# One-bank PSUM tiles instead of two-bank tiles for the accumulators of a gated MLP

## The chip, the cores and the metric

The kernel runs on one core of one Trainium2 chip. The core has five engines that run side by side and meet through semaphores: TensorE (matrix multiplication, "PE" in the profile), VectorE ("DVE"), ScalarE ("ACT"), GpSimd ("POOL") and SyncE ("SP", which issues transfers). TensorE writes its sums to PSUM, a memory of 8 banks; in this kernel a bank holds 512 fp32 values in each of 128 partitions. The metric is the device time of one execution in microseconds, as the median of several runs. Before the change it is 2559.89 us (three runs, 2557.91 to 2560.74).

## What is computed

One layer of a diffusion transformer over 512 latent tokens with 256 context tokens, in fp32: a modulated RMS norm, two attention mixers, an output projection, and a gated MLP, then a final norm. The change lies in the MLP, whose gate passes a convolution of width 3 over the tokens:

```python
g, u = jnp.split(h @ w_up, 2, axis=-1)            # h: 512 x 2048, w_up: 2048 x 11264
gp = jnp.pad(g, ((0, 0), (pad, pad), (0, 0)))
g = sum(gp[:, j:j + T] * conv_w[j] for j in range(CONV_W)) + conv_b
return (jax.nn.silu(g) * u) @ w_down              # w_down: 5632 x 2048
```

## The kernel before, in words

Tokens lie along the free dimension (T = 512 columns, halves h0 and h1 of HT = 256), features along the 128 partitions. Every fp32 product is made of three matmuls (`mm3`, L99 to L104): operands are split into a high part ("wh", cast on ScalarE) and the remainder ("wl", subtracted on VectorE), and high times high, high times low and low times high are added up in PSUM.

The 5632 features of the MLP are 44 tiles of 128. A tile needs two blocks of results, its gate g and its linear part u. Tiles 0 and 1 are made in `first_pair`, tile 2 by four plain jobs "u", the tiles 3 to 43 (`PAIRS`) by seven jobs each, ("p", ft, 0) to ("p", ft, 6), in a scheme of the Strassen kind: seven products of half size (8 weight blocks of 128 x 128 by 256 columns, 3 matmuls each, so 24 matmuls a job) take the place of eight. "A pair" in what follows is such a pair of g and u, one ft. Its seven products go to three accumulators: k = 0 to y, 1 to x, 2 to y, 3 to z, 4 to y, 5 to z, 6 to y. Readers take intermediate sums from them between the jobs:

- L999, ScalarE, after k = 0: copies y to m1
- L1002, ScalarE, after k = 2: copies y to u2
- L1005, ScalarE, and L1028, VectorE, after k = 3: copy z to m5, and g[h0] = x + m1
- L1033, VectorE, after k = 4: u[h1] = y + m5
- L1035, VectorE, after k = 5: u[h0] = z + u2
- L1007, ScalarE, after k = 6: copies y to g[h1]; then the convolution, SiLU and product with u (L806 to L828) follow, spread over the next pair's jobs

The down projection is spread among these jobs: after every fourth pair its 16 output blocks come in eight jobs "d", each of 24 matmuls with 512 columns into two PSUM tiles "b", at the places `DOWN_AFTER` (7, 8, 10, 11, 13, 14, 16, 17), counted as (ft % 4) * 7 + k. Their results go through ScalarE (L992, tile xs) and are added to the stream in DRAM by GpSimd's queue (L993).

The order is written out by hand (`manual_schedule`, L900) for TensorE, ScalarE, VectorE and SyncE, each a strict queue in this order (L1041 to L1055): for step i, the matmuls of job i are issued (`run`), then a sum of weight blocks where one is due (`weight_sum`, VectorE), the cast of the weights of job i + 2 (L945, ScalarE), the readers of job i - 1 (`act_after` on ScalarE, `vec_after` on VectorE), and the low part of the weights of job i + 2 (L951, VectorE). Weights come in by SyncE's queue in two rings of three buffers (L869).

The semaphores are not written by hand: the framework derives the waits from what each instruction reads and writes. A pool hands out tiles; tiles of one tag rotate through `bufs` buffers. Before the change PSUM is shared by two pools: `ps_s` (L60) with two tiles "s" of two banks, which has served since the kernel's start, and `ps_c` (L650) with four tiles "b" of one bank. A pair takes one tile s (L969): y is the first half of its first bank, z and x are the two halves of its second. Tile 2's jobs "u" use one tile s, g in its first bank and u in its second (L961).

Of the kernel before, what the change touches and what calls it, by code (L numbers as in the profile page):

```python
# [15 lines left out]
PSUM = bass.MemoryType.PSUM  # L16
# [36 lines left out]
def layer_kernel(ctx: ExitStack, tc: tile.TileContext, small, rope, c_row, cc_row, x_t, ctx_t, ada, ada_k,  # L53
# [3 lines left out]

    cst = ctx.enter_context(tc.tile_pool(name="cst", bufs=1))
    dram = ctx.enter_context(tc.tile_pool(name="dram", bufs=1, space=bass.MemoryType.DRAM))
    ps_s = ctx.enter_context(tc.tile_pool(name="ps_s", bufs=2, space=PSUM))  # L60
    ps_b = tc.alloc_tile_pool(name="ps_b", bufs=4, space=PSUM)

    n = [0]
# [5 lines left out]
    def s_tile():  # L69
        return ps_s.tile([P, 1024], F32, tag="s", name=nm("s"))  # L70
# [576 lines left out]
    mc.release()  # L647
    rp.release()
    ps_b.release()
    ps_b = ctx.enter_context(tc.tile_pool(name="ps_c", bufs=4, space=PSUM, reuse_waits="tile"))  # L650


    HT = T // 2
# [64 lines left out]
    db = sm.tile([P, 8], F32, name="db")  # L718
    ve.tensor_tensor(db, modx[:, 56:64], modx[:, 48:56], op=ALU.add)
    wo.release()  # L720

# [176 lines left out]
    with tc.manual_schedule(engines={mybir.EngineType.PE, mybir.EngineType.Activation, mybir.EngineType.DVE,  # L900
                                     mybir.EngineType.SP}):
        ra, rb = Ring(wp, "wr", 3, items_a), Ring(mm, "rb", 3, items_b)
        sums_, ready, live = {}, {}, {}

        def small(tag):
            return mm.tile([P, HT], F32, tag=tag, name=nm(tag), bufs=1)

        def weight_sum(ft, i):

            if ft >= NFT:  # L910
                return
            w12, w21, w22 = (rb.tiles.get((k, ft)) for k in ("w12", "w21", "w22"))
            if i in (1, 2):
                sums_[ft, i] = mm.tile([P, 1024], F32, tag="ws", name=nm("ws"), bufs=2)
            if i == 1:
                ve.tensor_tensor(sums_[ft, 1], w12, ra.tiles["w11", ft], op=ALU.subtract)
                ra.used(("w11", ft))
            elif i == 2:
                ve.tensor_tensor(sums_[ft, 2], w22, sums_[ft, 1], op=ALU.subtract)
                rb.used(("w22", ft))  # L920
            elif i == 3:
                ve.tensor_tensor(w12, w22, w12, op=ALU.subtract)
                rb.used(("w12", ft))
                rb.used(("w22", ft))
            else:
                ve.tensor_tensor(sums_[ft, 2], w21, sums_[ft, 2], op=ALU.subtract)
                rb.used(("w21", ft))

        def operand(job):

            if job[0] != "p":
                return ra.tiles[job], lambda: ra.used(job)
            ft, k = job[1:]
            if k == 0:
                return ra.tiles["w11", ft], lambda: ra.used(("w11", ft))
            if k in (2, 3, 6):
                return sums_[ft, 1 if k == 3 else 2], None
            key = ({1: "w21", 4: "w12", 5: "w22"}[k], ft)
            return rb.tiles[key], lambda: rb.used(key)

        def cast(i):
            if i < last:
                raw, done = operand(jobs[i])
                hi, lo = (wp.tile([P, 1024], F32R, tag=g, name=nm(g), bufs=3) for g in ("wh", "wl"))
                sc.copy(hi, raw)  # L945
                ready[i] = hi, lo, raw, done

        def low(i):
            if i < last:
                hi, lo, raw, done = ready[i]  # L950
                ve.tensor_tensor(lo, raw, hi.bitcast(F32), op=ALU.subtract)  # L951
                if done:
                    done()

        def run(i):
            job = jobs[i]
            wh, wl = ready.pop(i)[:2]
            w = [(wh[:, j * P:(j + 1) * P], wl[:, j * P:(j + 1) * P]) for j in range(8)]
            if job[0] == "u":
                if job[1] == 0:  # L960
                    live["s"] = s_tile()  # L961
                o = live["s"][:, (job[1] // 2) * 512:(job[1] // 2) * 512 + 512]
                for j in range(8):
                    kt = (job[1] % 2) * 8 + j
                    classical(o, kt, w[j], kt == 0, kt == KT - 1)
            elif job[0] == "p":
                ft, k = job[1:]
                if k == 0:
                    s = s_tile()  # L969
                    live[ft] = {"y": s[:, :HT], "z": s[:, 512:512 + HT], "x": s[:, 512 + HT:]}  # L970
                hs, out, start = ((h11, "y", True), (h21, "x", True), (t2, "y", False), (t1, "z", False),
                                  (t3, "y", False), (t4, "z", False), (h22, "y", False))[k]
                for j in range(8):
                    mm3(live[ft][out], w[j], hs[j], start and j == 0, j == 7, True)
            else:
                live["po"] = []
                for d in range(2):
                    po = b_tile()
                    for f in range(FC):
                        mm3(po, w[f * 2 + d], acts[job[1] * FC + f], f == 0, f == FC - 1)  # L980
                    live["po"].append(po)

        def act_after(i):

            job = jobs[i]
            if job[0] == "u" and job[1] == 3:
                live["t"] = gate_in(2, live["s"][:, :512])
            elif job[0] == "d":
                for d, po in enumerate(live["po"]):
                    dt = job[2] * 2 + d  # L990
                    x = mm.tile([P, T], F32, tag="xs", name=nm("xs"), bufs=XS)
                    sc.mul(x, po, modx[:, 80 + dt:81 + dt])  # L992
                    gp.dma_start(x1_d[dt], x, accum_op=ALU.add)  # L993
            elif job[0] == "p":
                ft, k = job[1:]
                v = live[ft]
                if k == 0:
                    v["m1"] = small("m1")
                    sc.copy(v["m1"], v["y"])  # L999
                elif k == 2:  # L1000
                    v["u2"] = small("u2")
                    sc.copy(v["u2"], v["y"])  # L1002
                elif k == 3:
                    v["m5"] = small("m5")
                    sc.copy(v["m5"], v["z"])  # L1005
                elif k == 6:
                    sc.copy(v["g"][:, h1], v["y"])  # L1007
                    v["t"] = gate_in(ft, v["g"])

        def vec_after(i):  # L1010
            job = jobs[i]
            if job[0] == "u" and job[1] == 3:
                silu(convolve(2, live["s"][:, :512], live["t"]))
            elif job == ("p", 3, 0):
                acts[2] = multiply(live["t"], live["s"][:, 512:])
            elif job == ("p", 3, 1):
                finish(live["t"], acts[2])
            if job[0] != "p":
                return
            ft, k = job[1:]  # L1020
            v, f = live[ft], live.get(ft - 1)
            if k == 2 and f:
                silu(convolve(ft - 1, f["g"], f["t"]))
            elif k == 3:
                if f:
                    acts[ft - 1] = multiply(f["t"], f["u"])
                v["g"] = mm.tile([P, T], F32, tag="g", name=nm("g"), bufs=1)
                ve.tensor_tensor(v["g"][:, h0], v["x"], v["m1"], op=ALU.add)  # L1028
            elif k == 4:
                if f:  # L1030
                    finish(f["t"], acts[ft - 1])
                v["u"] = mm.tile([P, T], F32, tag="u", name=nm("u"), bufs=1)
                ve.tensor_tensor(v["u"][:, h1], v["y"], v["m5"], op=ALU.add)  # L1033
            elif k == 5:
                ve.tensor_tensor(v["u"][:, h0], v["z"], v["u2"], op=ALU.add)  # L1035

        cast(0)
        low(0)
        cast(1)
        low(1)  # L1040
        for i, job in enumerate(jobs):  # L1041
            run(i)
            if job[0] == "p":
                ft, k = job[1:]
                if k in (0, 1, 2):
                    weight_sum(ft, k + 2)
                elif k == 6:
                    weight_sum(ft + 1, 1)
            elif job == ("u", 3):
                weight_sum(3, 1)  # L1050
            cast(i + 2)
            if i:
                act_after(i - 1)
                vec_after(i - 1)
            low(i + 2)  # L1055
        act_after(last - 1)
        f = live[NFT - 1]
        silu(convolve(NFT - 1, f["g"], f["t"]))
        acts[NFT - 1] = finish(f["t"], multiply(f["t"], f["u"]))
# [104 lines left out]
```

## Time and profile before

| | us |
|---|---|
| median of three runs | 2559.89 |
| lowest, highest | 2557.91, 2560.74 |
| the profiled execution | 2557.82 |
| its span (first to last instruction) | 2556.0 |
| TensorE matmul busy | 2420.2 |
| VectorE, ScalarE, GpSimd busy | 1643.2, 1087.3, 245.3 |

The profile is one execution. A line of its timeline reads: start and duration in us, engine, line of the kernel, operation, result <- operands (names of tiles without their numbers), shape, and in brackets how long the engine had been idle and whose end let it go on. A table of stretches gives, for each stretch of time, its length and the busy time of every engine with the number of instructions, then the granted clock of TensorE (1.00 is full), the share of the transfer engines and GB/s. Matmuls are pipelined: one is drawn longer than the distance to the next.

### The profile page before, as it was taken

What the parts mean: (1) busy time and instruction counts of PE and PEld (TensorE: products, weight loads), DVE (VectorE), ACT (ScalarE), POOL (GpSimd) and SP (SyncE); (2) the same over time, 40 slices, a digit from 0 to 9 for tenths busy, and PEclk for the clock granted to TensorE, in tenths of its full rate; (3) what the DMA queues carried; (4) which work ended last, traced back from release to release, by engine and by line L of the source; (5) the groups of instructions that cost most, each with busy time, mean ns of one, the idle gap of its engine ahead of it and who ended that gap; (6) DMA issues with size and microseconds to landing.
All of it is one profiled execution on the core that took longest, in us unless ns stands there. A gap on an engine that the chain in (4) does not pass through costs nothing.

```text
span 2556.0 us, 37051 instructions
## 1 busy us (share of the span) xinstructions
PE 2420.2 (95%) x14948; PEld 2104.7 (82%) x14948; DVE 1643.2 (64%) x2102; ACT 1087.3 (43%) x1660; POOL 245.3 (10%) x266
## 2 busy tenths in 40 slices
PE   7999999999899999999999999999999999999996
PEld 3778887777677788788989888988898889888886
DVE  4778876498787874675564646464646465656556
ACT  4342221365555622344444444444444444444443
POOL 0000000211100012000101010101010101010103
PEclk8999999999999999999999999999999999999998
DMA  7868888544311196224546363636363636454554
GB/s 276 289 211 321 328 331 303 174 130 135 111 41 46 66 335 220 96 97 118 133 114 151 93 163 100 161 97 161 102 146 108 150 100 147 118 134 127 136 165 149
DMA packets 131874, 407.78 MB, mean 160 GB/s; under 512 B 14451, under 2 KB 25203, under 8 KB 123251
## 3 DMA queue, kind: packets, MB, share of 16 engines
q1 hardware_dynamic: 106422, 356.11, 41.5%
q0 software_dynamic: 25280, 49.30, 11.0%
q8 instruction: 117, 1.92, 0.3%
q14 instruction: 55, 0.45, 0.1%
HBM read 335.88 MB, written 69.48 MB: 159 GB/s over the span
## 4 chain that ended last, share of the span: by engine, by line
PE 82%; DVE 8%; ACT 5%; issue 1%; DMA 1%; POOL 1%; SPq 0%; ACTq 0%; DVEq 0%; POOLq 0%
PE s L102 14%; PE s L103 13%; PE s L104 13%; PE b L103 10%; PE b L102 10%; PE b L104 10%; PE s L480 2%; ACT wh L945 2%; PE f L102 1%; PE pt L492 1%; DVE m L482 1%; PE f L103 1%; PE f L104 1%; DVE p L538 1%; PE b L217 1%
## 5 line engine op out<-in xcount | busy, mean ns | idle before, releaser
L102 PE MATMUL s<-a2k,wh 128*128 128x256 f32 (+1 forms) x1536 | 461.3, 301 | 24.9 <-DVE u L1033 16.4
L103 PE MATMUL s<-a2k,wh 128*128 128x256 f32 (+1 forms) x1536 | 458.9, 299 | 0.0
L104 PE MATMUL s<-a2k,wl 128*128 128x256 f32 (+1 forms) x1536 | 458.9, 299 | 0.0
L102 PEld LDWEIGHTS s<-a2k,wh 128*128 128x128 f32 x1536 | 293.9, 192 | 40.8 <-DVE u L1033 14.4
L103 PEld LDWEIGHTS s<-a2k,wh 128*128 128x128 f32 x1536 | 294.2, 192 | 9.0 <-issue 1.4
L104 PEld LDWEIGHTS s<-a2k,wl 128*128 128x128 f32 x1536 | 294.0, 191 | 8.5 <-DVE wl L951 0.8
L102 PE MATMUL b<-ah,wh 128*128 128x512 f32 (+1 forms) x768 | 286.3, 374 | 3.7 <-ACT ah L824 2.6
L103 PE MATMUL b<-al,wh 128*128 128x512 f32 (+1 forms) x768 | 287.0, 374 | 0.0
L104 PE MATMUL b<-ah,wl 128*128 128x512 f32 (+1 forms) x768 | 285.7, 372 | 0.0
L993 POOL DMA_DIRECT2D x_d<-xs x160 | 139.7, 1001 | 1258.9 <-ACT xs L992 1256.9
L78 ACT CAST wh<-wr 128x1024 fp32r<-128x1024 f32 (+2 forms) x134 | 132.7, 991 | 268.6 <-PE b L104 84.4
L951 DVE TENSOR_TENSOR wl<-ws,wh 128x1024 fp32r<-128x1024 f32 x123 | 150.4, 1223 | 136.6 <-ACT wh L945 136.6
L79 DVE TENSOR_TENSOR wl<-wr,wh 128x1024 fp32r<-128x1024 f32 (+2 forms) x134 | 156.6, 1169 | 104.3 <-ACT wh L78 100.7
L951 DVE TENSOR_TENSOR wl<-wr,wh 128x1024 fp32r<-128x1024 f32 x125 | 151.7, 1220 | 110.7 <-ACT wh L945 110.5
L945 ACT CAST wh<-rb 128x1024 fp32r<-128x1024 f32 x123 | 129.4, 1052 | 218.4 <-PE s L103 95.7
L945 ACT CAST wh<-wr 128x1024 fp32r<-128x1024 f32 x125 | 131.4, 1051 | 212.5 <-PE b L103 127.5
L945 ACT CAST wh<-ws 128x1024 fp32r<-128x1024 f32 x123 | 128.9, 1048 | 198.7 <-PE s L103 145.9
L951 DVE TENSOR_TENSOR wl<-rb,wh 128x1024 fp32r<-128x1024 f32 x123 | 150.1, 1221 | 96.8 <-ACT wh L945 96.8
L169 DVE CUSTOM_DVE_ANT_0 ada<-ada,cb,smt 128x2048 f32<-128x2048 f32 x64 | 151.2, 2365 | 58.7 <-DMA ada<-in_ada 58.4
L103 PE MATMUL s<-b2k,wh 128*128 128x256 f32 x656 | 185.6, 283 | 0.0
L102 PE MATMUL s<-b2k,wh 128*128 128x256 f32 x656 | 185.6, 283 | 0.0
L104 PE MATMUL s<-b2k,wl 128*128 128x256 f32 x656 | 185.4, 283 | 0.0
(317 smaller groups left out, 5450.7 us busy)
## 6 DMA issues: line engine op xcount, KB each, us to landing
ada<-in_ada SPq DMA_DIRECT2D x64, 1024.0 KB, 6.6
rb<-in_w_up SPq DMA_DIRECT2D x123, 512.0 KB, 4.3
wr<-in_w_dn SPq DMA_DIRECT2D x96, 512.0 KB, 3.2
x_d<-xs POOLq DMA_DIRECT2D x160, 256.0 KB, 5.9
wr<-in_w_up SPq DMA_DIRECT2D x53, 512.0 KB, 3.7
wr<-in_w_f SPq DMA_DIRECT2D x34, 512.0 KB, 6.2
adak<-in_ada_k SPq DMA_DIRECT2D x32, 512.0 KB, 6.2
ada<-in_ada SPq DMA_DIRECT2D x32, 512.0 KB, 6.5
```

The costliest lines, as they stand in the source:

```text
L78: sc.copy(dst_h, src)
L79: ve.tensor_tensor(dst_l, src, dst_h.bitcast(F32), op=ALU.subtract)
L102: pe.matmul(out, st[0], mv[0], start=start, stop=False, **kw)
L103: pe.matmul(out, st[0], mv[1], start=False, stop=False, **kw)
L104: pe.matmul(out, st[1], mv[0], start=False, stop=stop, **kw)
L169: ve.tensor_tensor_reduce(out=junk, in0=w, in1=vec, op0=ALU.mult, op1=ALU.add, scale=1.0, scalar=col("b_ada", j), accum_out=dst[:, j:j + 1])
L217: pe.matmul(acc[32 * c:32 * c + 32, :n], cpad[:, kt], src(kt), start=j == 0, stop=j == 3)
L480: pe.matmul(s[:, c0:c1], a, b[:, c0:c1], start=i == 0, stop=i == len(mms) - 1)
L482: ve.tensor_reduce(out=m, in_=s[:, :TT], axis=AX.X, op=ALU.max, negate=True)
L945: sc.copy(hi, raw)
L951: ve.tensor_tensor(lo, raw, hi.bitcast(F32), op=ALU.subtract)
L993: gp.dma_start(x1_d[dt], x, accum_op=ALU.add)
```

## The change

The MLP's accumulators become tiles of one bank each, from tags "y" and "z" with two buffers; x stays in z's bank. To make room the two PSUM pools are released after the output projection, and one new pool, `ps_m`, holds all eight banks: four tiles b, two y, two z. Jobs, matmuls, readers and their order stay as they are.

```diff
-    ps_s = ctx.enter_context(tc.tile_pool(name="ps_s", bufs=2, space=PSUM))
+    ps_s = tc.alloc_tile_pool(name="ps_s", bufs=2, space=PSUM)
...
-    ps_b = ctx.enter_context(tc.tile_pool(name="ps_c", bufs=4, space=PSUM, reuse_waits="tile"))
+    ps_b = tc.alloc_tile_pool(name="ps_c", bufs=4, space=PSUM, reuse_waits="tile")
...
     wo.release()
+    ps_b.release()
+    ps_s.release()
+    ps_b = ctx.enter_context(tc.tile_pool(name="ps_m", bufs=4, space=PSUM, reuse_waits="tile"))
...
                 if job[1] == 0:
-                    live["s"] = s_tile()
-                o = live["s"][:, (job[1] // 2) * 512:(job[1] // 2) * 512 + 512]
+                    live["s"] = [b_tile(g_, 2) for g_ in "yz"]
+                o = live["s"][job[1] // 2]
...
                 if k == 0:
-                    s = s_tile()
-                    live[ft] = {"y": s[:, :HT], "z": s[:, 512:512 + HT], "x": s[:, 512 + HT:]}
+                    y, z = (b_tile(g_, 2) for g_ in "yz")
+                    live[ft] = {"y": y[:, :HT], "z": z[:, :HT], "x": z[:, HT:]}
...
-                live["t"] = gate_in(2, live["s"][:, :512])
+                live["t"] = gate_in(2, live["s"][0])
...
-                silu(convolve(2, live["s"][:, :512], live["t"]))
+                silu(convolve(2, live["s"][0], live["t"]))
...
-                acts[2] = multiply(live["t"], live["s"][:, 512:])
+                acts[2] = multiply(live["t"], live["s"][1])
```

## The prediction

> **What bounds the kernel now.** I read the page first (busy shares, clock), then the waits of TensorE, then the timeline around one of those waits, then a table of stretches.
>
> ```profile
> span 2556.0 us, 37051 instructions
> PE 2420.2 (95%) x14948; PEld 2104.7 (82%) x14948; DVE 1643.2 (64%) x2102; ACT 1087.3 (43%) x1660; POOL 245.3 (10%) x266
> ```
>
> TensorE sets the time: 95% busy, VectorE next with 64%. So only what stands between matmuls can be won. The waits of TensorE, longest first (in total us, times, longest), begin with four rows, all ahead of a matmul into tile s, the MLP's accumulator:
>
> ```profile
> PE s L102 <- DVE g L1028: 18.4, 20, 0.9
> PE s L102 <- DVE u L1033: 16.4, 30, 0.6
> PE s L102 <- ACT m L999: 10.8, 21, 0.5
> PE s L102 <- ACT u L1002: 9.7, 21, 0.5
> ```
>
> Together 55.3 us in 92 waits. What they wait for are readers of the accumulator. A pair of tiles runs seven jobs of 24 matmuls, k = 0 to 6, into y, x, y, z, y, z, y (L971); y fills the first bank of s, z and x the halves of the second. After job i+1 is issued, the readers of job i's sum are (L1052 to L1054). The timeline at the end of job 1 of pair 3 (start, duration, engine, line, idle before and what ended it):
>
> ```profile
> 1143.12 0.28 PE L103 MATMUL s<-a2k,wh 128*128 128x256 f32 x1
> 1143.24 0.28 PE L104 MATMUL s<-a2k,wl 128*128 128x256 f32 x1
> 1143.55 0.37 ACT L999 COPY m<-s 128x256 f32<-128x256 f32 x1 [0.97 <-PE s L104]
> 1143.98 0.39 PE L102 MATMUL s<-tp,wh 128*128 128x256 f32 x1 [0.46 <-ACT m L999]
> 1144.20 0.28 PE L103 MATMUL s<-tp,wh 128*128 128x256 f32 x1
> 1144.32 0.29 PE L104 MATMUL s<-tp,wl 128*128 128x256 f32 x1
> ```
>
> L999 copies y, which job 0 had finished 24 matmuls (2.9 us) earlier. ScalarE stood idle for 0.97 us and began 0.03 us after the last matmul of job 1, which writes x, in the other bank. Then job 2, which writes y, waited for the copy. So a reader waits for everything already issued into its two-bank tile, not only for its own bank. Where a job of the down projection (tile b) comes between, it doesn't wait:
>
> ```profile
> 1715.63 0.28 PE L104 MATMUL s<-a2k,wl 128*128 128x256 f32 x1
> 1715.75 0.40 PE L102 MATMUL b<-ah,wh 128*128 128x512 f32 x1
> ...
> 1716.45 0.40 PE L102 MATMUL b<-ah,wh 128*128 128x512 f32 x1
> 1716.68 0.39 PE L103 MATMUL b<-al,wh 128*128 128x512 f32 x1
> 1716.91 0.39 PE L104 MATMUL b<-ah,wl 128*128 128x512 f32 x1
> 1717.14 0.39 PE L102 MATMUL b<-ah,wh 128*128 128x512 f32 x1
> ```
>
> ```profile
> 1715.83 1.05 ACT L945 CAST wh<-wr 128x1024 fp32r<-128x1024 f32 x1 [0.66 <-PE s L103]
> 1716.79 0.36 ACT L999 COPY m<-s 128x256 f32<-128x256 f32 x1
> ```
>
> Here the same copy follows its predecessor on ScalarE at once, at 1716.79, while matmuls into b run. They keep their 0.23 us from start to start through the copy, so such a read costs TensorE nothing visible.
>
> **The change part by part.** With y and z as tiles of their own, a reader of y waits for the last job into y alone. Five reads change (the job they wait for now, in brackets): L999 (1), L1002 (3), L1005 and L1028 (4), L1033 (5), L1035 (6). Nobody waits for L1035. The other four hold up the next job; which pairs have them follows from DOWN_AFTER. Down jobs follow k = 0, 1, 3, 4, 6 in pairs with ft % 4 = 1 and k = 0, 2, 3 in those with ft % 4 = 2. That leaves all four stalls in the 21 pairs with remainder 0 or 3 (3, 4, 7, 8, ... 43), and L1033's alone in 10 pairs with remainder 2: 31. The counts of the waits (20, 30, 21, 21) are these, short by one record in two rows.
>
> What a stall costs is more than its row. Unstalled matmuls of 256 columns start every 0.12 us, though each is drawn 0.28 long, so idle counted from the drawn end leaves out 0.16; and the second matmul after a stall starts 0.22 after the first, 0.10 more. In the rows above: 1143.24 to 1144.20 is 0.96, unstalled 0.24, so 0.72 against a wait of 0.46. First sum: 55.3 + 92 x 0.26 = 79.2 us. Second sum, from one pair without down jobs, cut from one L1002 to the next:
>
> ```profile
> core 0: us, PE busy (x) PEld busy (x) DVE busy (x) ACT busy (x) POOL busy (x), PEclk, DMA share, GB/s
> 1678.04:1701.64 23.60, 21.18 (x169) 20.37 (x168) 16.56 (x19) 10.18 (x14) 0.00 (x0) 1.00 0.28 91
> ```
>
> Its 168 matmuls take 168 x 0.12 = 20.16 us; 23.60 - 20.16 = 3.44 is lost. 21 x 3.44 = 72.2, plus 10 x (0.6 + 0.26) = 8.6 for the pairs with L1033 alone (0.6 is that row's longest): 80.8. I take **80 us**.
>
> Does something else come next? Three reads need to be done by the time the next job into their bank begins, one whole job (24 x 0.12 = 2.88 us) later: L999 and L1002 stand on ScalarE behind one cast of 1.05 us, L1033 on VectorE. The narrowest is L1028, which reads x behind L1005's read of z, and job 5 then writes z:
>
> ```profile
> 1678.16 0.37 ACT L1002 COPY u<-s 128x256 f32<-128x256 f32 x1 [1.95 <-PE s L104]
> 1678.43 0.64 ACT L818 ACTIVATE t<-t 128x512 f32<-128x512 f32 x1
> 1678.96 1.04 ACT L945 CAST wh<-ws 128x1024 fp32r<-128x1024 f32 x1
> 1681.76 0.37 ACT L1005 COPY m<-s 128x256 f32<-128x256 f32 x1 [1.75 <-PE s L104]
> ```
>
> ```profile
> 1679.10 0.69 DVE L822 TENSOR_TENSOR t<-t,u 128x512 f32<-128x512 f32 x1 [0.98 <-ACT t L818]
> 1682.16 0.42 DVE L1028 TENSOR_TENSOR g<-s,m 128x256 f32<-128x256 f32 x1 [2.38 <-ACT m L1005]
> ```
>
> After the change L1002 and L818 move into job 3, so the cast can start with job 4, when its buffer comes free (the cast at 1715.83 above began 0.08 us after the matmuls of the next job): 1.05 + 0.37 + 0.42 and three hand-overs of about 0.05 (1681.76 + 0.37 to 1682.16 is 0.03) give L1028's end 2.0 us into job 4, 0.9 before job 5. L822, ahead of it on VectorE, comes earlier as L818 does. If that cover is gone, this stall stays:
>
> ```profile
> 1681.44 0.28 PE L104 MATMUL s<-b2k,wl 128*128 128x256 f32 x1
> 1682.64 0.39 PE L102 MATMUL s<-tp,wh 128*128 128x256 f32 x1 [0.92 <-DVE g L1028]
> ```
>
> 1.20 from start to start, 1.08 more than unstalled, and 0.10 for the second matmul: 21 x 1.18 = 25 us. As a whole VectorE has 16.6 us of work in a pair of 20.2, ScalarE 10.2. The transfers of such a pair, 91 GB/s now, become 91 x 23.60 / 20.16 = 107; the page's 40 slices show up to 335:
>
> ```profile
> GB/s 276 289 211 321 328 331 303 174 130 135 111 41 46 66 335 220 96 97 118 133 114 151 93 163 100 161 97 161 102 146 108 150 100 147 118 134 127 136 165 149
> ```
>
> [...]
>
> Pools: releasing ps_c and ps_s and opening ps_m moves the first tile b of the MLP to banks that the third group of the output projection left. Its first matmuls are these:
>
> ```profile
> 1050.46 1.02 PE L678 MATMUL b<-ss,ones 128*128 128x512 f32 x2
> 1052.06 3.70 PE L682 MATMUL b<-sq,ones 128*128 128x512 f32 x8 [0.57 <-ACT sq L681]
> ```
>
> L682 waits for data until 1052.06 in any case, so an earlier L678 gains nothing, and one held back to there costs under 1.1 us (its own length); I take 0. Buffers: y and z have two each, as s had; a pair takes over those of two pairs before, whose last read is a whole pair (over 20 us) past: 0. The tiles b keep four.
>
> **The sum.** The profiled execution took 2557.82 us (span 2556.0 and 1.8 around it), 2.07 under the median of 2559.89. 2557.8 - 80 = 2478 for it, and 2480 against the median: 3.1% less.
>
> **The rivals.**
> *A late chain at L1028.* If ScalarE or VectorE reaches L1005 or L1028 0.9 us later than I worked out, job 5 keeps its stall; with all of it kept the gain is 80 - 25 = 55: 2505. For it: four instructions in a row on two engines. Against: every one of them moves earlier, none is added. Chance 0.10.
> *The wait is not the tile's.* If readers wait for whatever job TensorE was given last, splitting the tile changes nothing: 2560. [...] For it: each of the stalled reads does stand behind the latest job. Against: the copy at 1716.79, under a down job. Chance 0.05.
> *Slower: the clock.* With the pauses gone, TensorE streams without a break through the pairs, and the granted clock could fall there. Some of its matmuls into s (start of the first and the last at the end of the times):
>
> ```profile
> L102 PE MATMUL s<-b2k,wh x656: 280/283/283, 1145.2 to 2478.3; 128*128 128x256 f32 x164
> ```
>
> Less 80, that is 1253 us. It decides from 80 / 1253 = 6.4%: below 0.94 the kernel is slower than before; at 0.90 it takes 2480 + 1253 x 0.11 = 2618. Against it, two stretches, one of them already as dense as the MLP would become:
>
> ```profile
> 100.00:200.00 100.00, 97.78 (x771) 76.51 (x770) 74.47 (x136) 42.54 (x77) 0.00 (x0) 1.00 0.71 249
> 1500.00:2000.00 500.00, 478.21 (x3289) 443.27 (x3288) 292.40 (x306) 221.62 (x303) 50.63 (x58) 1.00 0.49 125
> ```
>
> 97.8% busy at a clock of 1.00. [...] Chance 0.03.
>
> **How the numbers follow.** The forecast, 2480, has 0.82. Its own spread: the two sums differ by 1.6, the runs of before by 2.8, a leftover of 0.1 us at each of the 94 places would be 9, and up to 8 more could come from the end of the MLP (ScalarE and VectorE arrive there earlier): 2472 to 2490. The range reaches on to the first rival: 2472 to 2506, about 0.9 of the chance. 0.2%, 5 us, is about what a measurement of this kernel can tell from no change. Faster by more: 0.82 + 0.10 = 0.92; within: 0.05; slower: 0.03.
>
> **What would show it.** Right: L999, L1002 and L1033 start in the middle of the next job, not 0.03 us after it; the four rows of TensorE's waits are gone or under 2 us each; a pair without down jobs takes 20.2 us instead of 23.60; the stretch of the MLP is some 80 us shorter at a clock of 1.00, and all before it as long as now. L1028 goes on waiting for L1005 (both read one tile). Wrong: readers that still begin with the end of a job of the other tile, a new releaser in front of matmuls into y or z, casts L945 that end a matmul's wait, or matmuls that start more than 0.12 us apart while a reader is busy.

## The result, and the profile after

| | before | after |
|---|---|---|
| median, us | 2560.27 | 2481.17 |
| lowest, highest | 2557.91, 2560.74 | 2480.08, 2482.73 |
| runs | 4 | 4 |
| the profiled execution | 2557.82 | 2480.95 |

The kernel is faster by 79.1 us: the ratio is 0.9693, with a 95% interval of 0.9676 to 0.9710. The forecast was 2480, a gain of 80. (The kernel before was run once more, so its median is 2560.27 here and not 2559.89. The added lines move the kernel's later lines down: the readers L999, L1002, L1005, L1028, L1033, L1035 are L1002, L1005, L1008, L1031, L1036, L1038 after the change, and the cast L945 is L948.)

The first lines of the page of the changed kernel:

```profile
span 2479.2 us, 37121 instructions
PE 2399.1 (97%) x14948; PEld 2101.6 (85%) x14948; DVE 1646.3 (66%) x2102; ACT 1088.0 (44%) x1660; POOL 243.2 (10%) x266
```

The same number of matmuls is done in less time. The waits of TensorE between the first and the last matmul of the accumulators (1105 to 2407 us) are two rows, both from the start, the jobs "u"; the longer one stood in the kernel before as well, with 4.4 us:

```profile
PE z L102 <- ACT wh L948: 4.2, 1, 4.2
PE z L104 <- DVE wl L954: 0.5, 1, 0.5
```

All four rows of before, 92 waits, are gone. How the readers come to lie, in one pair without down jobs. First ScalarE, then VectorE, then TensorE (start, duration, engine, line, idle before):

```profile
1644.53 0.36 ACT L1002 COPY m<-y 128x256 f32<-128x256 f32 x1
...
1650.29 0.37 ACT L1005 COPY u<-y 128x256 f32<-128x256 f32 x1
...
1652.27 1.05 ACT L948 CAST wh<-ws 128x1024 fp32r<-128x1024 f32 x1 [1.08 <-PE z L103]
1653.22 0.37 ACT L1008 COPY m<-z 128x256 f32<-128x256 f32 x1
```

```profile
1653.62 0.42 DVE L1031 TENSOR_TENSOR g<-z,m 128x256 f32<-128x256 f32 x1 [1.38 <-ACT m L1008]
...
1655.70 0.42 DVE L1036 TENSOR_TENSOR u<-y,m 128x256 f32<-128x256 f32 x1
```

```profile
1644.46 0.28 PE L104 MATMUL z<-a2k,wl 128*128 128x256 f32 x1
1644.58 0.28 PE L102 MATMUL z<-a2k,wh 128*128 128x256 f32 x1
1644.70 0.28 PE L103 MATMUL z<-a2k,wh 128*128 128x256 f32 x1
1644.82 0.28 PE L104 MATMUL z<-a2k,wl 128*128 128x256 f32 x1
...
1654.90 0.28 PE L104 MATMUL y<-b2k,wl 128*128 128x256 f32 x1
1655.02 0.28 PE L102 MATMUL z<-tp,wh 128*128 128x256 f32 x1
```

At 1644.53 ScalarE reads y while job 1 writes x into z, 0.12 us from start to start, without a pause. L1031 ends at 1654.04 and job 5 begins at 1655.02, 0.12 after the last matmul of job 4. L1036 then reads y inside job 5. The table of stretches, whose columns are those shown before, gives the pair and the middle of the MLP:

```profile
1644.53:1664.69 20.16, 20.16 (x170) 20.16 (x170) 16.65 (x19) 10.29 (x15) 0.00 (x0) 1.00 0.34 106
```

```profile
1500.00:2000.00 500.00, 500.00 (x3479) 469.22 (x3478) 308.81 (x322) 238.07 (x324) 57.31 (x66) 1.00 0.54 136
```

The pair takes 20.16 us, from one copy L1002 to the next, where one without down jobs took 23.60; TensorE is busy for all of the 500 us, 478 before, and its clock is 1.00.

What the profile of each says on the whole stage is in one row of the accumulator's tile: start of the first and of the last of the matmuls, s before, y after:

```profile
L102 PE MATMUL s<-a2k,wh x1344: 277/283/797, 1100.0 to 2482.0; 128*128 128x256 f32 x190, 128*128 128x512 f32 x2
```

```profile
L102 PE MATMUL y<-a2k,wh x672: 277/283/396, 1105.6 to 2406.3; 128*128 128x256 f32 x166, 128*128 128x512 f32 x2
```

1382.0 us before, 1300.7 after: 81.3 less. The profiled execution of after came to this point 5.6 us later than that of before, in stages that the change leaves as they are, which is why the two spans differ by only 76.8. That start is not the change's doing: in the profiles below it lies between 1100.4 and 1106.2, at 1104.7 and 1100.4 in two kernels as slow as before and at 1102.6 in one as fast as after. Most of it is the clock. Ahead of that point the granted clock stood at 0.50 for 30.7 us in all in the profile of before and for 41.0 us in that of after; the difference, at half speed, is worth up to 5.1 us. So the length of the accumulators' stage is the cleaner measure of what a kernel gains, and most runs below have it beside the time.

### The profile page after: what moved, and what is told of

It reads as the page before. It is cut to its first block, busy times and chain, and to the rows that moved or that the text cites. A ratio compares the mean times of both kernels' runs of the same rounds, so it can differ in the third digit from the quotient of the medians.

```text
span 2479.2 us, 37121 instructions
## 1 busy us (share of the span) xinstructions
PE 2399.1 (97%) x14948; PEld 2101.6 (85%) x14948; DVE 1646.3 (66%) x2102; ACT 1088.0 (44%) x1660; POOL 243.2 (10%) x266
## 4 chain that ended last, share of the span: by engine, by line
PE 83%; DVE 9%; DMA 4%; ACT 2%; issue 2%; POOL 1%; SPq 0%; DVEq 0%; ACTq 0%; POOLq 0%
PE b L103 9%; PE b L102 9%; PE b L104 9%; PE y L103 6%; PE y L104 6%; PE y L102 6%; PE z L104 5%; PE z L103 5%; PE z L102 5%; PE s L102 3%; PE s L103 3%; PE s L104 3%; PE s L480 3%; DMA ada<-in_ada 2%; PE f L102 1%
## 5 line engine op out<-in xcount | busy, mean ns | idle before, releaser
L948 ACT CAST wh<-wr 128x1024 fp32r<-128x1024 f32 x125 | 131.1, 1049 | 242.3 <-PE b L103 123.3
L948 ACT CAST wh<-rb 128x1024 fp32r<-128x1024 f32 x123 | 129.1, 1050 | 239.2 <-PE b L103 67.5
L948 ACT CAST wh<-ws 128x1024 fp32r<-128x1024 f32 x123 | 128.9, 1048 | 163.0 <-PE b L103 52.9
L102 PE MATMUL z<-a2k,wh 128*128 128x256 f32 (+1 forms) x672 | 191.4, 285 | 4.2 <-ACT wh L948 4.2
L104 PE MATMUL z<-a2k,wl 128*128 128x256 f32 (+1 forms) x672 | 191.8, 285 | 0.5 <-DVE wl L954 0.5
L103 PE MATMUL z<-a2k,wh 128*128 128x256 f32 (+1 forms) x672 | 191.5, 285 | 0.0
L103 PE MATMUL y<-a2k,wh 128*128 128x256 f32 (+1 forms) x672 | 191.0, 284 | 0.0
L104 PE MATMUL y<-a2k,wl 128*128 128x256 f32 (+1 forms) x672 | 191.0, 284 | 0.0
L102 PE MATMUL y<-a2k,wh 128*128 128x256 f32 (+1 forms) x672 | 191.0, 284 | 0.0
L104 PEld LDWEIGHTS b<-ah,wl 128*128 128x128 f32 x768 | 144.7, 188 | 25.6
L102 PEld LDWEIGHTS b<-ah,wh 128*128 128x128 f32 x768 | 144.8, 189 | 24.7 <-ACT ah L827 1.8
L103 PEld LDWEIGHTS b<-al,wh 128*128 128x128 f32 x768 | 145.0, 189 | 22.2 <-DVE al L831 0.2
```

The costliest lines, as they stand in the source:

```text
L102: pe.matmul(out, st[0], mv[0], start=start, stop=False, **kw)
L103: pe.matmul(out, st[0], mv[1], start=False, stop=False, **kw)
L104: pe.matmul(out, st[1], mv[0], start=False, stop=stop, **kw)
```

## Experiments

The theory: a reader waits for every matmul issued before it into its tile, whichever bank it reads; tiles of one bank cut that to the bank. Rivals: the new pool did it; or the readers' waits are no path to TensorE at all. In the expectations "the changed kernel" has 2481 us.

**The pool alone.** The new pool of eight banks, with the pair's accumulators in a tile of two banks as before:

```diff
-                    y, z = (b_tile(g_, 2) for g_ in "yz")
-                    live[ft] = {"y": y[:, :HT], "z": z[:, :HT], "x": z[:, HT:]}
+                    s = ps_b.tile([P, 1024], F32, tag="s", name=nm("s"), bufs=2)
+                    live[ft] = {"y": s[:, :HT], "z": s[:, 512:512 + HT], "x": s[:, 512 + HT:]}
```

> The new pool of eight banks, but the accumulators of a pair again in one tile s of two banks. Theory (a reader waits for all that is issued into its tile): all 92 stalls are back, 2560 us, within 5. Rival (the gain came with the new pool, its banks or its waits at reuse): 2481 us.

Measured: 2562.84 us, 1.0007 of before (0.9998 to 1.0016). The waits of TensorE:

```profile
PE s L102 <- DVE g L1031: 18.4, 20, 0.9
PE s L102 <- DVE u L1036: 16.4, 30, 0.6
PE s L102 <- ACT m L1002: 10.7, 21, 0.5
PE s L102 <- ACT u L1005: 9.7, 21, 0.5
```

They are the rows of before to a tenth, and the accumulators' stage takes 1381.6 us. The pool gives nothing; the whole gain is the splitting of the tile.

**x beside y.** Same pool, same tiles, but x in the other half of y's bank (job 1 then adds into a bank that job 0 has begun, and job 3 begins z's):

```diff
-                    live[ft] = {"y": y[:, :HT], "z": z[:, :HT], "x": z[:, HT:]}
+                    live[ft] = {"y": y[:, :HT], "z": z[:, :HT], "x": y[:, HT:]}
```

> Pool and tiles of the changed kernel, but x lies in the second half of y's bank instead of z's. Theory: the copy of y after k = 0 again stands behind job 1, which writes x into the same tile, in the 21 pairs without a down job there; 21 x 0.78 = 16 us, so 2497 us, within 3, and a row of TensorE waiting for that copy, 21 times; the read of x after k = 3 now waits for job 4 into y, but nothing is held up by it. Rival (pool or banks as such): 2481 us.

Measured: 2493.10 us, 0.9734 of before (0.9718 to 0.9751), 11.9 more than the changed kernel instead of 16, and so a little outside the expected 2494 to 2500. The rows (TensorE's wait, then VectorE's):

```profile
PE y L102 <- ACT m L1002: 9.7, 21, 0.5
```

```profile
DVE g L1031 <- PE y L104: 63.0, 21, 3.6
```

Exactly the one stall that was foretold is back, at its 21 places, and the read of x now waits for job 4 into y, at no cost. From the first to the last matmul into the accumulators it is 1315.8 us in the profile (1100.8 to 2416.6), 15.1 more than after. That is the price of this stall by the prediction's way of counting, 21 x (0.46 + 0.26) = 15.1; the 0.78 of the expectation was too high. The medians' 11.9 has an uncertainty of some 6 us by the two intervals, and the profile starts this stage 4.8 us earlier than that of after.

**x by itself.** A tile and a bank for x, and three buffers for the tiles b (job 3 then begins z's bank, and the fourth sum of `first_pair` uses the tile x; these lines are not shown):

```diff
-                    y, z = (b_tile(g_, 2) for g_ in "yz")
-                    live[ft] = {"y": y[:, :HT], "z": z[:, :HT], "x": z[:, HT:]}
+                    y, z, x = b_tile("y", 2), b_tile("z", 2), b_tile("x", 1)
+                    live[ft] = {"y": y[:, :HT], "z": z[:, :HT], "x": x[:, :HT]}
```

> x gets a tile and bank of its own (one buffer; tiles b have three buffers instead of four). Theory: VectorE's read of x no longer waits for ScalarE's read of z (41 waits, 56.6 us gone), and since TensorE has no pause left in the pairs, the time stays at 2481 us, within 3. Rival (the waits that are left still cost something): 5 us or more faster.

Measured: 2481.61 us, 0.9687 of before (0.9673 to 0.9702), no different from after; the stage takes 1300.5 us. In the changed kernel VectorE's waits hold this row, and here there is none from that copy:

```profile
DVE g L1031 <- ACT m L1008: 56.6, 41, 1.7
```

So even two reads, of different halves of a tile, wait for each other (here the tile is one bank, so this run doesn't tell which of the two it goes by), and what is left of such waits after the change costs nothing.

**Using up the slack.** How late may L1031 be? The copy L1008 ahead of it, done again and again:

```diff
-                    sc.copy(v["m5"], v["z"])
+                    for _ in range(9):
+                        sc.copy(v["m5"], v["z"])
```

> The changed kernel with the copy of z after k = 3 done nine times over instead of once (the same copy, the same result). Theory (the chain behind it ends about 1.0 us before job 5): eight more copies of 0.27 to 0.37 us each are 2.2 to 3.0 us, so job 5 is held up for 1.2 to 2.0 us and 0.26 for the restart in the 21 pairs without a down job there: 31 to 47 us, 2512 to 2528 us. Rival (this read isn't on a path to TensorE): 2481 us.

Measured: 2555.27 us, 0.9973 of before (0.9964 to 0.9982): nearly all of the gain is gone, 27 to 43 us more than expected. ScalarE, TensorE's wait, and TensorE behind one of the pauses:

```profile
1572.43 3.60 ACT L1009 COPY m<-z 128x256 f32<-128x256 f32 x9
```

```profile
PE z L102 <- DVE g L1032: 44.0, 21, 2.2
```

```profile
1574.10 0.28 PE L104 MATMUL y<-b2k,wl 128*128 128x256 f32 x1
1576.55 0.39 PE L102 MATMUL z<-tp,wh 128*128 128x256 f32 x1 [2.16 <-DVE g L1032]
...
1577.36 0.28 PE L102 MATMUL z<-b2k,wh 128*128 128x256 f32 x1
1577.48 0.28 PE L103 MATMUL z<-b2k,wh 128*128 128x256 f32 x1
...
1577.99 0.42 PE L103 MATMUL z<-b2k,wh 128*128 128x256 f32 x1
1578.21 0.42 PE L104 MATMUL z<-b2k,wl 128*128 128x256 f32 x1
1578.42 0.41 PE L102 MATMUL z<-b2k,wh 128*128 128x256 f32 x1
```

Two things were mis-sized. Eight more copies take 3.60 - 0.37 = 3.23 us, 0.40 each, not 0.27 to 0.37, and the pause is 2.45 us from start to start, 2.33 more than unstalled: 3.23 - 2.33 = 0.9 us were free, as the prediction had worked out. And some time after the pause the matmuls stand 0.21 us apart instead of 0.12: the clock has fallen. The table of stretches has it at 0.50 for 3.41 us, here with the stretch before, in which the pause lies:

```profile
1574.24:1577.65 3.41, 1.25 (x11) 1.11 (x10) 1.58 (x3) 3.13 (x7) 0.00 (x0) 1.00 0.00 0
1577.65:1581.06 3.41, 3.41 (x18) 3.41 (x18) 3.18 (x4) 0.05 (x1) 0.00 (x0) 0.50 0.02 5
```

That follows on 16 of the 20 long pauses, for 16 or so matmuls, at 1.5 us each time. 20 x (2.33 + 0.10) + 16 x 1.5 = 73 us, and 2481 + 73 = 2554; the accumulators' stage is 75.4 us longer than after. So that the copy isn't the only thing measured, three more sizes:

> The changed kernel with the copy of z after k = 3 done three times. Eight more took 3.23 us, 0.40 each, and held job 5 up for 2.32 us, so 0.91 us of slack were used up first. Theory (nothing is lost until the slack is gone): two more are 0.81 us, within the slack: 2481 us, within 3. Rival (each delay of the readers costs its own length): 21 x 0.81 = 17 us, 2498 us.

> The same copy done six times: 5 x 0.40 - 0.91 = 1.1 us of pause at 21 places, plus 0.10 for the restart: 21 x 1.2 = 25 us, 2506 us, if a pause as short as in the kernel before (1.20 us from start to start) leaves the clock alone. If the clock falls after each such pause too, as it did after 16 of 20 pauses of 2.44 us, another 24 us: 2530 us.

> The same copy done eight times: a pause of 1.9 us (2.04 us from start to start) at 21 places, 21 x 2.0 = 42 us, 2523 us with the clock left alone, and up to 1.5 us more for each pause after which it falls (2555 us if after all). Where it falls, matmuls of 256 columns stand 0.21 us apart for some 16 of them.

| more copies | us | of before | accumulators' stage, against after | pause, start to start | pauses with a fall of the clock |
|---|---|---|---|---|---|
| 2 | 2477.10 | 0.9672 (0.9658 to 0.9687) | -0.3 | none | none |
| 5 | 2503.67 | 0.9780 (0.9764 to 0.9797) | +24.8 | 1.23 | 0 of 21 |
| 7 | 2535.74 (one run) | | +57.8 | 2.03 | 10 of 20 |
| 8 | 2555.27 | 0.9973 (0.9964 to 0.9982) | +75.4 | 2.44 | 16 of 20 |

Two more, 0.81 us, are free: the rival by which each delay costs its own length falls. The time is 4.1 us under the changed kernel's, 1.1 more than the 3 allowed for; the two intervals meet, the stage is as long as after, and it started 3.0 us earlier in the profile. Five cost 22 us in the time and 24.8 in the stage for 25 expected, seven 55 and 57.8 for 42 and 10 falls at 1.5, 57 in all. The slack of 0.9 us is shown from both sides.

**Do writers wait as well?** Could the kernel before have been freed by order alone, with the reader issued ahead of the next job? Two-bank tiles, and only the copy of y after k = 0 moved, first to the end of its own step:

```diff
+            if job[0] == "p" and job[2] == 0:
+                act_after(i)
```

> The kernel before, two-bank tiles, with the copy of y after k = 0 issued before job 1 instead of after it. If writers, too, wait for all that is issued into and out of their tile: the stall moves from the start of job 2 to that of job 1 and stays as long, 2560 us, within 3. If only readers wait by the tile and writers go by what they overlap: the stall of this copy is gone, 21 x 0.78 = 16 us, 2544 us.

Measured: 2617.06 us, 1.0225 of before (1.0210 to 1.0241), which neither expected. The profile has why: TensorE waits longer for that copy than before, and the cast that is now ahead of it on ScalarE waits for a weight sum of VectorE:

```profile
PE s L102 <- ACT m L999: 50.0, 21, 2.4
```

```profile
1835.28 1.04 ACT L945 CAST wh<-ws 128x1024 fp32r<-128x1024 f32 x1 [5.54 <-DVE ws L919]
1836.23 0.36 ACT L1007 COPY g<-s 128x256 f32<-128x256 f32 x1
1836.62 0.81 ACT L806 ACTIVATE t<-g,smt 128x512 f32<-128x512 f32 x1
1837.34 0.35 ACT L999 COPY m<-s 128x256 f32<-128x256 f32 x1
```

```profile
1835.03 0.28 PE L104 MATMUL s<-a2k,wl 128*128 128x256 f32 x1
1837.75 0.39 PE L102 MATMUL s<-a2k,wh 128*128 128x256 f32 x1 [2.44 <-ACT m L999]
```

The last matmul of job 0 ended at 1835.31, and y was complete 2 us before the copy at 1837.34. Job 1 waited for the copy, so the stall moved; but it grew to 2.7 us from start to start, and 14 of these 21 pauses brought a fall of the clock: 20 x 2.70 + 14 x 1.5 = 75 us in place of 15, and the accumulators' stage is 59.9 us longer than before. Put ahead of that cast instead, straight after `run(i)`:

> The kernel before, two-bank tiles, with the copy of y after k = 0 issued straight after job 0, ahead of the cast behind which it got stuck in the run before. If a writer of x waits for a reader of y in the same tile: the stall stands ahead of job 1 instead of job 2, as long as it was (0.79 us from start to start, 21 times), 2560 us, within 4. If writers go by the bank: no stall for this copy, 2544 us.

Measured: 2560.37 us, 0.9999 of before (0.9989 to 1.0008). The accumulators' stage takes 1381.8 us, and the four rows are back to their sizes, this one with a different job behind it:

```profile
PE s L102 <- DVE g L1028: 18.4, 20, 0.9
PE s L102 <- DVE u L1033: 16.4, 30, 0.6
PE s L102 <- ACT m L999: 9.7, 21, 0.5
PE s L102 <- ACT u L1002: 9.7, 21, 0.5
```

One of these places, ScalarE and then TensorE from the end of job 0 on:

```profile
1669.78 0.37 ACT L999 COPY m<-s 128x256 f32<-128x256 f32 x1 [5.61 <-PE s L104]
```

```profile
1669.46 0.28 PE L104 MATMUL s<-a2k,wl 128*128 128x256 f32 x1
1670.21 0.39 PE L102 MATMUL s<-a2k,wh 128*128 128x256 f32 x1 [0.46 <-ACT m L999]
...
1673.07 0.28 PE L104 MATMUL s<-a2k,wl 128*128 128x256 f32 x1
1673.18 0.28 PE L102 MATMUL s<-tp,wh 128*128 128x256 f32 x1
```

Job 1 (1670.21), which writes x in one bank, waited for a read of y in the other, and job 2 (1673.18) follows without a pause. Writers go by the tile too, so with two-bank tiles none of the three places tried for this reader avoids the stall; the place only chooses the job that has it. A job of the down projection between the two does avoid it, as in the pairs that have one there (21 waits in 41 pairs).

## Why the prediction was right

- *The waits are the tile's.* Right: shown by the pool alone (no gain), by x beside y (the foretold stall and no other) and by the two orders of the reader (a writer waits as well). The rival that a reader waits for the latest job whatever its tile falls with the first profile of after: L1002 at 1644.53 reads under job 1.
- *The price of a stall, row + 0.26.* Right: 79.2 and 80.8 by the two sums; the stage lost 81.3 us in the profile, the median 79.1. That the median meets the forecast to about 1 us is in part luck: the stages ahead, which the prediction took to stay as long as they were, differ between the two profiled executions by 5.6 us. The stage is the better test, and there the sum is off by 1.3. Had one taken the rows of the waits alone, 55 us, a third would have been missed: a wait is counted from the end at which a matmul is drawn, 0.28 us after its start, where the next one starts after 0.12; and the second matmul after it comes 0.22 us after the first instead of 0.12 (1143.98 to 1144.20 in before).
- *Nothing is next.* Right: 0.9 us of slack at L1028 by the working, 1655.02 - 1654.04 = 1.0 in the profile, 0.9 by the added copies. VectorE's work in a pair, 16.6 us, fits in 20.16. One new wait was not foreseen, and is as harmless:

```profile
ACT wh L948 <- DVE ws L922: 51.3, 20, 3.7
```

  The cast for job 2 waits for a weight sum, which VectorE now reaches later in the pair; TensorE has no wait behind it.
- *The pool's first tiles cost 0.* Right: the pool alone is at 1.0007.
- *The clock.* The rival had the sign turned about. In after TensorE is busy for all of the 500 us from 1500 to 2000, and its clock is 1.00 from 1139.77 to 2464.13. It fell behind pauses, when they were made 2 us long: 10 of 20 of 2.03 us. Behind those of before in the pairs, 20 of 1.20 us from start to start and one of 1.34 at the longest, it never did: 1.00 from 1140 to 2480.

## What to carry to other kernels

When a reader of PSUM begins with the end of a matmul that doesn't write what it reads, look at what shares its tile: waits here went by the tile for readers and writers alike, so sums with different due times want tiles of their own, and moving the reader, in the orders tried, only moved the stall. Price a stall of TensorE from start to start of its matmuls, not from the listed wait. And work out how late the next chain may be: here 0.9 us were free, and beyond them each added copy cost its length, and more once pauses reached 2 us (seven copies cost 55 us, 42 expected with the clock left alone).

## What the runs showed of the hardware

The granted clock of TensorE fell behind pauses of 2 us and more in the pairs, though not behind all: after none of 21 of 1.23 us from start to start, 10 of 20 of 2.03, 16 of 20 of 2.44 and 14 of 20 of 2.72. The mean granted clock of these four profiled executions is 0.989, 0.982, 0.977 and 0.979, that of after 0.988. It fell not at the pause: at the place shown above job 5 begins at 1576.55 and the stretch at 0.50 at 1577.65, nine matmuls later; it is 3.41 us long, some 16 matmuls 0.21 us apart. Outside the pairs, two longer pauses of before have such a stretch of 3.41 us behind them: 4.67 us from 1125.57 on, with 0.50 from 1130.21, and 2.92 us from 2485.45 on, with 0.50 from 2488.72. One of 1.83 us in after, from 2410.89 on, has none. Why 20 of the 60 pauses of 2.03 us and more brought no fall is not shown.

In both profiles, that of before and that of after, the starts of the stretches at 0.50 lie whole multiples of 3.413 us apart: 1058.53, 1130.21 and 2488.72 us in before, 21 and 398 times, and 1064.67 and 1136.35 us in after, 21 times.

The read of one bank of PSUM by ScalarE while TensorE wrote another cost neither anything visible: in after the matmuls keep their 0.12 us from start to start through the copy at 1644.53, and the copy takes 0.36; the 41 copies of y after k = 0 have a median of 0.366 us there and of 0.365 in before.
